# Queries in a pool of their own, column sums behind their conversions, and only the sums kept in DRAM: one change to a hybrid attention and SSD layer

## The chip, the core and the metric

The kernel runs on one core of a Trainium2 chip. The metric is the device time of that core in microseconds; a time stands for the median of several executions, and one further execution was taken with the profiler. The engines are named as in the profile: PE (matmul, with PEld for its weight loads), DVE (vector), ACT (scalar), POOL (GpSimd) and SP, which here only issues transfers. ACT and POOL issue transfers too, in the order of their other instructions.

## The reference

One decoder layer over x of 2048 positions by 1024 columns, in float32. A single projection gives queries, keys, values, two gates, the input of a convolution, and the step sizes of the SSD. Sixteen heads of causal attention with ALiBi bias are taken over windows of 128 steps at dilations 1, 4 and 16; beside them runs a Mamba-2 SSD scan over chunks of 128. Both branches are gated, normalized, put side by side and projected back:

```python
proj = jnp.einsum('bsd,de->bse', x, w_in[layer])
q, k, v, z_att, z_ssm, xbc, dt_raw = jnp.split(proj, list(SPLITS), axis=-1)
...
y_att = rms_norm(y_att.reshape(Bsz, S, D_ATT) * jax.nn.silu(z_att), att_norm_g[layer])
xbc = jax.nn.silu(causal_depthwise_conv(xbc, conv_w[layer], conv_b[layer]))
...
y = ssd_chunked(xs_h, dt, a, bm, cm) + d_skip * xs_h
y_ssm = rms_norm(y * jax.nn.silu(z_ssm), ssm_norm_g[layer])
out = jnp.einsum('bse,ed->bsd', jnp.concatenate([y_att, y_ssm], axis=-1), w_out[layer])
x = layer_norm(alpha * x + out, ln_g[layer], ln_b[layer])
```

## The kernel before

**Precision.** A float32 product is made of three matmuls: each operand is split into a high part (rounded to the faster fp32r type by ACT) and the rest (a subtraction on POOL or DVE), and high by high, high by low and low by high are summed in PSUM.

**Stages.** First the values are projected (L122 to L214). Then comes the product phase (L590 to L703), about half of the time: all other columns of the projection, and between them the convolution, the SSD and preparations for later. The attention follows (L706 on), eight pairs of heads, each over three dilations; last comes the output projection with the norm.

**The product phase.** It uses a Strassen-like scheme. A *job* is a block of 256 columns by one half of the tokens, and `products` (L289) makes it from seven products instead of eight; each product is 12 matmuls of 128x512. The token side has seven combinations of quarters of x (`LEFT`, L85), each a high and a low tile of 1 MB, read by `token_side` (L221) from DRAM; all fourteen lie in SBUF and change only when the half changes. The column side has seven combinations of the weight's quarters A11, A12, A21, A22: `column_load` (L234) brings the raw quarters (256 KB each) into tiles `wr`, `column_side` (L247) forms sums in place (`tt`, L250, on DVE) and splits each of the seven (`two`: the cast on ACT, L254, and the subtraction on POOL, L255) into a tile `w` of 512 KB. The order of the seven is A11, S1 = A21 + A22, A12, the new A11, the new A12, A22, A21; numbers 1, 3, 4 and 6 of them, counted from 0, are sums. Pool `wp` has seven `w` tiles, so a new one fits when the product that reads the old one is done.

There are 44 jobs in three phases: 10 with the first half of the tokens (phase 0: convolution inputs "c" and SSD gates "s"), 22 with the second half (phase 1: the same, and from job 19 on queries "q", keys "k" and attention gates "z", the list `rest`), and 12 with the first half again (phase 2: `rest`). The columns of phase 2 were used in phase 1, so there `column_side` stores its seven tiles into `d_wc` (L257, on SP), and in phase 2 `column_reload` (L269) reads all seven back (L274, on POOL) without ACT or DVE.

**The order.** PE, DVE, ACT and POOL run in the order of the program text. `products` calls `flush` after each product; `after(n, f)` puts work n flushes ahead, so a *step* is one product. Columns of the next job are prepared from step 2 to step 8, the raw quarters of the one after next loaded at steps 3, 4, 6 and 7. `keep` (L301, L303) copies a product from PSUM on ACT, `put` (L306, L311) adds on DVE, and `fin` stores or goes on one step later. PSUM has five tiles `pp` for this, four used by a job.

Other work hangs on the same steps: `sums_part` (L103) forms the token combinations of the second half in jobs 0 to 3; `wout_load` (L639) brings pieces of the output weight, split three steps later by `split_w` (L115) into two buffers `wot` and stored on SP; `copy_v` (L477) rearranges the values in DRAM; in phase 1 `conv_tile` (L376) reads a convolution input `U` (two buffers) at step 0 and 3 of its job, `conv_steps` (L392) runs it on ACT (L397), DVE (three taps, L400) and ACT (L406). From job 23 on 32 SSD units (chunk, group) are placed at `spots` (L615): 13 of them 63/13 steps apart, then 19 at 4.1 steps. A unit has six stages, a step each: `ssd1` (L497) transposes on PE, masks the product of B and C with `tri` on DVE (L507), makes eight ramps on ACT (L513) and then copies B's transpose on ACT (L517); `ssd2` (L519) takes the exponential and multiplies by the mask; the last ones are matmuls and gates, and `d_us` is stored (L576).

**Memory.** Pools grow from both sides of SBUF. On the right, the SSD's tiles (`sd`, 36 KB a partition) follow the convolution's. When the product phase ends, the attention's pools lie over them: on the right `qk0` and `qk1`, the keys of two pairs of heads (16 KB each), on the left `io`, with the queries (`qh`, `ql`) first, which puts them over the `w` tiles. `load_qk` (L724) reads queries and keys, high and low, on POOL's queue in the order qh, kh, ql, kl.

## Time and profile before

| | us |
|---|---|
| median of three runs | 2279.07 (2272.51 to 2279.48) |
| the profiled execution | 2279.57 |
| its span, first to last instruction | 2277.8 |
| values projected until | 209.4 |
| product phase | 209.4 to 1336.3 |
| attention from | 1353.8 |

The mean granted clock of PE over the span is 0.948. The page gives, for each engine, its busy time and the number of its instructions; the stretches give the same for a part of the span; the waits name the engine and line that stood still, what released it, the total, how often, and the longest. A row with L255 means line 255 of the kernel; a row with "<-" in its tiles reads as out <- in. Idle time of an engine is a cost only where the chain that ends last runs through it.

### The profile page before, as it was taken

To read this page: it belongs to the slowest core of one execution; us is meant where nothing else is said; L and a number is where in the kernel's file an instruction comes from. 1 tells how busy PE (TensorE), PEld (TensorE's weight loads), DVE (VectorE), ACT (ScalarE), POOL (GpSimd) and SP (SyncE) were. 2 spreads that over 40 slices of the span, in tenths; PEclk is the share of its full clock that TensorE was granted. 3 is DMA by queue.
4 is the path that set the end of the run, shared out by engine and by line. 5 is a ranking of instruction groups with operands and counts; after the bars stand their busy time and mean duration, and the time that the engine had idled before them with its cause. 6 is when DMAs were issued, how large, how long until landed. Compare 5 with 4: busy or idle time off the path is not lost.

```text
span 2277.8 us, 38897 instructions
## 1 busy us (share of the span) xinstructions
PE 2088.7 (92%) x13824; PEld 1729.8 (76%) x13824; DVE 1368.8 (60%) x3141; ACT 1132.2 (50%) x2967; POOL 1017.3 (45%) x815
## 2 busy tenths in 40 slices
PE   7999789879898899988999979999999985999998
PEld 7998667657777677766888858888888864888886
DVE  3421554437778667743555537888888865565554
ACT  3321443325445566643655637888888861222221
POOL 2113343446565565653444431366677771232221
PEclk9999889989999999998999978999999997999999
DMA  9989666876667999899999973577777799422220
GB/s 333 367 313 334 229 230 240 294 297 197 206 207 254 331 358 342 322 364 386 292 316 303 304 257 120 162 199 211 220 218 219 218 318 273 152 99 100 80 91 35
DMA packets 280561, 557.51 MB, mean 245 GB/s; under 512 B 45360, under 2 KB 136624, under 8 KB 264368
## 3 DMA queue, kind: packets, MB, share of 16 engines
q1 hardware_dynamic: 206496, 291.81, 39.8%
q0 software_dynamic: 35152, 173.03, 21.2%
q10 hardware_dynamic: 38720, 90.20, 12.3%
q8 instruction: 109, 1.79, 0.3%
q14 instruction: 84, 0.69, 0.1%
HBM read 357.42 MB, written 214.30 MB: 251 GB/s over the span
## 4 chain that ended last, share of the span: by engine, by line
PE 40%; DMA 12%; DVE 5%; ACT 4%; issue 2%; POOL 1%; ACTq 0%; SPq 0%; DVEq 0%; POOLq 0%
PE S L795 6%; PE N L844 6%; PE T L824 6%; PE S L1004 3%; PE S L1006 3%; PE S L1005 3%; DMA zt<-d_zs 3%; PE pp L294 2%; PE pp L296 2%; PE pp L298 2%; PE T L1004 2%; PE T L1005 2%; PE T L1006 2%; ACT P L811 1%; DVE P L803 1%
## 5 line engine op out<-in xcount | busy, mean ns | idle before, releaser
L255 POOL TENSOR_TENSOR w<-wr,w 128x512 fp32r<-128x512 f32 x224 | 354.3, 1599 | 282.4 <-ACT w L254 223.2
L811 ACT ACTIVATE P<-P,st 128x256 f32<-128x256 f32 (+1 forms) x768 | 345.1, 451 | 95.2 <-DVE st L803 94.4
L803 DVE CUSTOM_DVE_ANT_0 P<-S,tb 128x256 f32<-128x256 f32 (+1 forms) x768 | 235.2, 362 | 97.8 <-PE S L795 67.2
L826 DVE COPY PT<-T 128x512 f32<-128x512 f32 (+1 forms) x304 | 196.6, 677 | 1.5 <-PE T L824 1.5
L824 PE MATMUL T<-ident,P 128*128 128x128 f32 x1200 | 179.6, 287 | 5.9 <-DVE PT L826 5.9
L303 ACT COPY ev<-pp 128x512 f32<-128x512 f32 x176 | 102.2, 581 | 156.4 <-PE pp L298 103.6
L844 PE MATMUL N<-PT,v 128*64 128x128 f32 x2400 | 176.5, 284 | 0.0
L250 DVE TENSOR_TENSOR wr<-wr 128x512 f32<-128x512 f32 x128 | 129.9, 1015 | 71.9 <-POOL w L255 54.0
L254 ACT CAST w<-wr 128x512 fp32r<-128x512 f32 x224 | 136.2, 618 | 62.7 <-DVE wr L250 21.2
L844 PEld LDWEIGHTS N<-PT,v 128*64 128x64 f32 x2400 | 129.3, 138 | 33.3 <-issue 22.6
L824 PEld LDWEIGHTS T<-ident,P 128*128 128x128 f32 x1200 | 130.1, 142 | 30.8 <-DVE PT L826 7.3
L811 ACT ACTIVATION_READ_ACCUMULATOR P<-P,st 128x1 f32 x768 | 143.7, 187 | 0.0
L911 POOL TENSOR_TENSOR wb<-num,wb 128x2048 f32<-128x2048 f32 x21 | 96.3, 4586 | 100.1 <-DMA wb<-d_wd 58.8
L311 DVE TENSOR_TENSOR ev<-pp,ev 128x512 f32<-128x512 f32 x152 | 100.7, 682 | 60.8 <-PE pp L298 41.7
L795 PE MATMUL S<-kh,qp 64*128 64x256 f32 (+1 forms) x1024 | 126.4, 306 | 0.0
L981 DVE TENSOR_REDUCE tb<-P 128x128 f32<-128x1024 f32 x32 | 64.0, 2000 | 85.5 <-PE N L1010 45.3
L400 DVE SCALAR_TENSOR_TENSOR acc<-U,cw,acc 128x2048 f32<-128x2048 f32 x36 | 106.6, 2961 | 6.0 <-ACT acc L397 5.5
L294 PE MATMUL pp<-TT3h,w 128*128 128x512 f32 x176 | 78.0, 443 | 34.8 <-ACT ev L303 33.2
L795 PEld LDWEIGHTS S<-kh,qp 64*128 64x128 f32 x1024 | 88.8, 188 | 22.0 <-issue 20.9
L146 PE MATMUL pp<-vh,xh 128*128 128x256 f32 (+1 forms) x320 | 90.8, 290 | 14.5 <-ACT xh L169 14.5
L351 DVE SCALAR_TENSOR_TENSOR ev<-ev 128x512 f32<-128x512 f32 x64 | 60.2, 955 | 66.5 <-ACT ev L350 66.4
L513 ACT ACTIVATE mt<-csb,cs 128x128 f32<-128x128 f32 x256 | 78.5, 390 | 36.8 <-DMA csb<-d_cs 34.2
(362 smaller groups left out, 5994.5 us busy)
## 6 DMA issues: line engine op xcount, KB each, us to landing
d_wc<-w SPq DMA_DIRECT2D x84, 512.0 KB
w<-d_wc POOLq DMA_DIRECT2D x84, 512.0 KB, 7.4
wr<-w ACTq DMA_DIRECT2D x120, 256.0 KB
v<-d_v POOLq DMA_DIRECT2D x24, 1024.0 KB, 7.0
wb<-d_wd SPq DMA_DIRECT2D x48, 512.0 KB
csb<-d_cs ACTq DMA_DIRECT2D x32, 512.0 KB
st<-xT SPq DMA_DIRECT2D x31, 512.0 KB
d_v<-vt SPq DMA_DIRECT2D x16, 512.0 KB
```

Of the source, the lines that this page charges most:

```text
L250: tt = lambda o, a, b, op=OP.subtract: nc.vector.tensor_tensor(q[o], q[a], q[b], op=op)
L254: nc.scalar.copy(t[:, 0], q[nm])
L255: nc.gpsimd.tensor_tensor(t[:, 1], q[nm], t[:, 0].bitcast(F32), op=OP.subtract)
L294: nc.tensor.matmul(ps, w[:, 0, k], th[:, k], start=start and k == 0, stop=False, skip_group_check=not start)
L795: nc.tensor.matmul(ov(sp[h][:, 256 * b:256 * b + w]), A["q"][d][x][hr, blk], kv(A["k"][y][hr]), start=(m == 0), stop=(m == 2))
L803: nc.vector.tensor_tensor_reduce(P[:, h, b, 256 - w:256], sp[h][:, c0:c0 + w], tab[:, h, tab.shape[2] - w:], 1.0, 3.0e38, OP.add, OP.min, ...
L811: nc.scalar.activation(p, p, AF.Exp, bias=stat(A, 0, d, h, blk), scale=-1.0, accum_out=stat(A, 1, d, h, blk))
L824: nc.tensor.transpose(tp[:, h, b], P[:, h, b, 128 * which:128 * which + 128], ident)
L826: nc.vector.tensor_copy(pt[:, :, bl[0]:2], tp[:, :, bl[0]:2])
L844: nc.tensor.matmul(nm[64 * h:64 * h + 64, bq * 128:bq * 128 + 128], v[:, k, 64 * h:64 * h + 64], pts[which][:, h, b], start=(f or not whic ...
L1004: nc.tensor.matmul(ps, uh[:, e, :], wh, start=(e == 0), stop=False)
L1005: nc.tensor.matmul(ps, uh[:, e, :], wl, start=False, stop=False)
```

## The change

- `column_reload` reads only the four sums back from `d_wc`; the other three of a job (A11, A12, A22) are made from raw quarters as in `column_side`. So `column_load` runs for phase 2 too, with three quarters (`part`), on ACT's queue. `column_side` stores the sums alone.
- `column_side` has nine steps from step 0 on: A11 is converted at step 1 (2 before), A12 at step 2 (4 before); the in-place sums stay at steps 2, 4 and 5 and the other conversions where they were. `slot` takes the buffers in the old order. The four reloads come at steps 2, 4, 5 and 7 instead of 1, 3, 4 and 6.
- From job 11 on the first `conv_tile` of a job runs at step 5 of the job before.
- `sums_part` runs in jobs 1 to 4 instead of 0 to 3.
- `wot` has four buffers instead of two, and a piece of the output weight comes every 5/3 steps instead of 7/4.
- In the SSD, the copy of B's transpose moves in front of the ramps, and the masking from `ssd1` to `ssd2`; the later units stand 4 steps apart instead of 4.1.
- The queries get a pool `qq` on the right, between the two pools of keys, where the SSD's tiles lay.

```diff
-        def column_load(ct0, ct1, queue=nc.gpsimd):
+        def column_load(ct0, ct1, queue=nc.gpsimd, part=False):
...
+            if part:
+                return q, [lambda: load("A11", ct0, 0), lambda: load("A12", ct0, 1), lambda: load("A22", ct1, 1)]
             return q, [first, lambda: load("A12", ct0, 1), lambda: load("A22", ct1, 1), lambda: load("A21", ct1, 0)]
+
+        SUMS = (1, 3, 4, 6)
...
-            def two(nm):
-                t = wp.tile([128, 2, 4, 128], F32R, name="w")
+            def slot():
+                W.append(wp.tile([128, 2, 4, 128], F32R, name="w"))
+
+            def two(i, nm):
+                t = W[i]
                 nc.scalar.copy(t[:, 0], q[nm])
                 nc.gpsimd.tensor_tensor(t[:, 1], q[nm], t[:, 0].bitcast(F32), op=OP.subtract)
-                if save is not None:
-                    nc.sync.dma_start(d_wc[save, len(W)], t.bitcast(F32).rearrange("p a k c -> p (a k c)"))
-                W.append(t)
+                if save is not None and i in SUMS:
+                    nc.sync.dma_start(d_wc[save, i], t.bitcast(F32).rearrange("p a k c -> p (a k c)"))
...
-            steps = [[sums, lambda: two("A11")], [lambda: two("S1")],
-                     [lambda: tt("A11", "S1", "A11"), lambda: two("A12")],
-                     [lambda: tt("A12", "A12", "A11"), lambda: two("A11")],
-                     [lambda: two("A12")], [lambda: two("A22")], [lambda: two("A21")]]
+            steps = [[], [slot, lambda: two(0, "A11")], [sums, slot, slot, lambda: two(2, "A12")],
+                     [lambda: two(1, "S1")], [lambda: tt("A11", "S1", "A11")],
+                     [lambda: tt("A12", "A12", "A11"), slot, lambda: two(3, "A11")],
+                     [slot, lambda: two(4, "A12")], [slot, lambda: two(5, "A22")], [slot, lambda: two(6, "A21")]]
...
-        def column_reload(u):
+        def column_reload(u, q):
...
-            def two():
+            def step(i):
                 t = wp.tile([128, 2, 4, 128], F32R, name="w")
-                nc.gpsimd.dma_start(t.rearrange("p a k c -> p (a k c)"), d_wc[u, len(W)])
+                if i in SUMS:
+                    nc.gpsimd.dma_start(t.rearrange("p a k c -> p (a k c)"), d_wc[u, i])
+                else:
+                    nm = {0: "A11", 2: "A12", 5: "A22"}[i]
+                    nc.scalar.copy(t[:, 0], q[nm])
+                    nc.gpsimd.tensor_tensor(t[:, 1], q[nm], t[:, 0].bitcast(F32), op=OP.subtract)
                 W.append(t)
-            return W, [two] * 7
+            return W, [lambda: None] + [lambda i=i: step(i) for i in range(7)]
...
-            nc.vector.tensor_tensor(pb[:, 256:384], pb[:, 128:256], tri, op=OP.mult)
             if n < 15:
+                A["bs"] = bs = [sd.tile([128, 128], F32R, name=f"bs{p}", bufs=2) for p in "hl"]
+                nc.scalar.copy(bs[0], pb[:, 0:128])
                 A["xde"] = xde = sd.tile([128, 512], F32, name="xde")
...
-            if n < 15:
-                A["bs"] = bs = [sd.tile([128, 128], F32R, name=f"bs{p}", bufs=2) for p in "hl"]
-                nc.scalar.copy(bs[0], pb[:, 0:128])
...
             nc.scalar.activation(mt, mt, AF.Exp, scale=-1.0)
+            nc.vector.tensor_tensor(pb[:, 256:384], pb[:, 128:256], tri, op=OP.mult)
...
-        spots = [7 * 23 + 63 * i // 13 if i < 13 else 7 * 32 + (41 * (i - 13)) // 10 for i in range(32)]
+        spots = [7 * 23 + 63 * i // 13 if i < 13 else 7 * 32 + 4 * (i - 13) for i in range(32)]
...
-                after(3, lambda: split_w(j // 2, j % 2, raw, sums.tile([128, 2, 512], F32R, name="wot", bufs=2)))
+                after(3, lambda: split_w(j // 2, j % 2, raw, sums.tile([128, 2, 512], F32R, name="wot", bufs=4)))
             for j in range(16):
-                later.setdefault(7 * 5 + 1 + 7 * j // 4, []).append(lambda j=j: wout_load(16 + j))
+                later.setdefault(7 * 5 + 1 + 5 * j // 3, []).append(lambda j=j: wout_load(16 + j))
...
-                    for j in range(7):
-                        after(j + (0 if ph2 == 2 else 2), prep[j])
+                    for j, f in enumerate(prep):
+                        after(j, f)
...
-                if m + 2 < len(jobs) and jobs[m + 2][0] < 2:
-                    q2, steps_ = column_load(*cts[m + 2], nc.scalar)
+                if m + 2 < len(jobs):
+                    q2, steps_ = column_load(*cts[m + 2], nc.scalar, jobs[m + 2][0] == 2)
                     for n, f in zip((3, 4, 6, 7), steps_):
                         after(n, f)
+                if 10 < m + 1 < len(jobs) and jobs[m + 1][1][0] == "c":
+                    Un = [None]
+                    after(5, lambda i=jobs[m + 1][1][1], U=Un: (U.clear(), conv_tile(i, U)))
...
-                if m < 4:
+                if 1 <= m < 5:
                     for c in range(4):
-                        after(1 + c, lambda c=c, k=m: sums_part(sums, 1, k, raws[k], c))
-                    if m < 3:
-                        after(5, lambda k=m + 1: raws.__setitem__(k, sums_load(sums, 1, k)))
+                        after(1 + c, lambda c=c, k=m - 1: sums_part(sums, 1, k, raws[k], c))
+                    if m < 4:
+                        after(5, lambda k=m: raws.__setitem__(k, sums_load(sums, 1, k)))
...
-        qk = [c2.enter_context(tc.tile_pool(name=f"qk{i}", bufs=1, side="right", reuse_waits="tile"))
-              for i in range(2)]
+        qk = [c2.enter_context(tc.tile_pool(name="qk0", bufs=1, side="right", reuse_waits="tile"))]
+        qq = c2.enter_context(tc.tile_pool(name="qq", bufs=1, side="right", reuse_waits="tile"))
+        qk.append(c2.enter_context(tc.tile_pool(name="qk1", bufs=1, side="right", reuse_waits="tile")))
...
-                t = (io if x[0] == "q" else qk[pr % 2]).tile([128, NR, NJ], F32R, name=x, bufs=1)
+                t = (qq if x[0] == "q" else qk[pr % 2]).tile([128, NR, NJ], F32R, name=x, bufs=1)
```

## What the change will do, told before it was run

> **What bounds the kernel now.** I read the page's busy times first.
>
> ```profile
> PE 2088.7 (92%) x13824; PEld 1729.8 (76%) x13824; DVE 1368.8 (60%) x3141; ACT 1132.2 (50%) x2967; POOL 1017.3 (45%) x815
> ```
>
> TensorE leads, but a busy PE is not a PE at its peak, so the product phase was cut into stretches: the 44 jobs start where the timeline shows their first matmul on the tile TB11. The columns are the stretch, then busy time and instructions of PE, weight load, DVE, ACT and POOL, the granted clock, the DMA share and GB/s.
>
> ```profile
> 209.40:321.30 111.90, 90.18 (x342) 71.84 (x343) 60.13 (x92) 45.18 (x78) 46.69 (x38) 0.85 0.69 233
> 340.70:378.80 38.10, 38.10 (x170) 31.54 (x169) 15.96 (x19) 15.27 (x27) 16.25 (x12) 1.00 0.63 211
> 378.80:404.80 26.00, 22.01 (x85) 17.68 (x84) 12.12 (x12) 9.55 (x18) 11.20 (x8) 0.87 0.80 277
> 423.80:456.00 32.20, 24.10 (x86) 18.86 (x86) 13.26 (x13) 8.39 (x15) 14.28 (x16) 0.84 0.88 319
> 456.00:496.80 40.80, 27.47 (x86) 19.72 (x85) 8.00 (x11) 7.33 (x13) 14.96 (x18) 0.79 1.02 384
> 496.80:761.00 264.20, 240.99 (x1010) 193.56 (x1009) 206.72 (x163) 135.45 (x215) 158.16 (x94) 0.96 0.68 218
> 761.00:1004.00 243.00, 226.85 (x1184) 186.40 (x1182) 161.15 (x235) 156.77 (x317) 149.30 (x116) 0.96 0.93 337
> 1004.00:1058.50 54.50, 36.12 (x126) 25.88 (x125) 14.13 (x27) 16.60 (x35) 18.37 (x25) 0.75 1.08 413
> 1058.50:1292.10 233.60, 230.54 (x1301) 191.80 (x1300) 122.39 (x232) 136.42 (x281) 107.50 (x124) 1.00 0.93 304
> 1292.10:1317.00 24.90, 24.39 (x143) 20.15 (x141) 13.54 (x25) 13.21 (x29) 6.13 (x10) 1.00 1.09 369
> 1336.30:1353.80 17.50, 0.47 (x2) 0.32 (x3) 1.29 (x2) 1.23 (x2) 10.44 (x16) 0.58 1.00 370
> 1353.80:1385.60 31.80, 31.80 (x219) 25.38 (x220) 14.86 (x88) 19.21 (x84) 4.19 (x8) 0.50 0.19 70
> 1401.60:1433.40 31.80, 31.80 (x390) 26.59 (x388) 26.61 (x109) 24.37 (x96) 7.99 (x13) 1.00 0.22 72
> ```
>
> The second row is the yardstick: jobs 5 and 6 run without a gap, 38.1 / 2 = 19.05 us a job, 2.72 us a product. Job 42 (1292.1 to 1317.0) carries SSD units every 4.1 products, 7 / 4.1 = 1.71 of them, and takes 24.9: a unit costs PE (24.9 - 19.05) / 1.71 = 3.4 us. What a stretch takes beyond jobs and units is lost time:
>
> - jobs 0 to 3: 111.9 - 76.2 = 35.7
> - job 7: 26.0 - 19.05 = 7.0; job 9: 32.2 - 19.05 = 13.1; job 10, where all token tiles change: 40.8 - 19.05 = 21.8
> - jobs 11 to 22: 264.2 - 228.6 = 35.6
> - jobs 23 to 31 with 13 units: 243.0 - 171.5 - 44.2 = 27
> - job 32, the second change of token tiles: 54.5 - 19.05 - 5.8 = 30
> - jobs 33 to 41 with 15.4 units: 233.6 - 171.5 - 52.4 = 10
> - from the last product to the steady attention: 17.5
>
> Some 198 us, then, are in reach, 180 of them inside the phase of 1336.3 - 209.4 = 1127; the other 947 us of it are matmuls, and attention and output behind them are not touched. The waits say what ended the gaps (engine and line, releaser: total us, times, longest). Jobs 0 to 3:
>
> ```profile
> PE pp L294 <- ACT ev L303: 21.6, 4, 6.9
> DVE st L108 <- DMA st<-xT: 16.7, 2, 12.6
> ```
>
> Jobs 7 to 9:
>
> ```profile
> ACT wot L117 <- DMA d_wo<-wot: 42.5, 7, 12.5
> POOL w L255 <- ACT w L254: 36.5, 11, 8.5
> PE pp L294 <- ACT ev L303: 12.1, 3, 5.1
> POOL w L255 <- issue: 11.8, 2, 10.5
> ```
>
> Jobs 11 to 22:
>
> ```profile
> ACT U L406 <- DVE acc L400: 50.9, 10, 6.9
> DVE wr L250 <- POOL w L255: 39.8, 14, 6.3
> PE pp L294 <- ACT ev L303: 20.7, 10, 4.3
> ACT acc L397 <- DMA U<-d_cu: 20.4, 3, 7.5
> ```
>
> Everywhere PE waits for ACT's copy out of PSUM (L303), and ACT, which works in order, is stuck at something else: a store that has not landed, a convolution input, a DVE that itself waits for POOL.
>
> **The change part by part.**
>
> *Sums of the second token half, one job later.* No work is removed. Job 0 loses its four steps and with them the 12.6 us wait; the block then was loaded a whole job earlier. Job 4, clean until now, receives a set. Job 0's stall at its sixth product, some 8 us of its 11.7, goes; job 4 gets a stall like job 3's, 25.2 - 19.05 = 6 at most, and jobs 1 to 3 keep theirs. Bounds 0 and 12; near the middle I take **6 us**.
>
> *Output-weight staging, four buffers for two, a load every 5/3 products for 7/4.* The store of a buffer now has 4 x 1.67 x 2.72 = 18 us to land, against 9.5. A wait of at most 12.5 behind 9.5 means stores of up to 22, so most of the 42.5 us goes, not all. Job 7 gives 7. Job 9 gives up to 13; and since POOL hung on ACT in front of the token loads (10.5 us in the wait on "issue", where no releaser was found), those loads start earlier too. But they are fourteen tiles of 128x2048 fp32, 14.7 MB, at the 384 GB/s of job 10's row 38 us with nothing else to move: transfers take over there, and I give jobs 9 and 10 together 13 instead of 35. Sum **20 us**, bounds 5 and 34.
>
> *Convolution inputs from the step after the sixth product of the job before, not at the start of their own.* A lead of two products, 5.4 us, meets waits of at most 7.5 (20.4 us in three). The reset of the tile moves with it on POOL, and waits there for the store of the tile's last user; behind it on POOL are conversions that PE needs five products later. *In-place sums two products behind the conversions*: A11 is converted at step 1 instead of 2, A12 at 2 instead of 4, while the sums that overwrite them stay at 4 and 5. The 39.8 us that DVE spends on POOL here go; DVE is at 206.7 of 264.2 busy in this stretch and keeps ACT waiting 50.9 us (L406 on L400). What is late next is DVE itself. The new wait: A12's buffer comes free just as its cast is issued, so ACT can stand up to one product, 2.72 us, once a job; behind it is only the copy of the next product, which PE has not made yet. Bounds: 0 and the 35.6 lost; I take **14 us**, two fifths, since DVE's own load remains.
>
> *SSD and stores in jobs 23 to 31.*
>
> ```profile
> d_wc<-w SPq DMA_DIRECT2D x84, 512.0 KB
> w<-d_wc POOLq DMA_DIRECT2D x84, 512.0 KB, 7.4
> wr<-w ACTq DMA_DIRECT2D x120, 256.0 KB
> ```
>
> Of 84 stores 48 stay: 36 x 0.52 = 18.9 MB less of writing, in a stretch at 337 GB/s and share 0.93, which is 56 us of transfers over some thirteen jobs. The copy of B comes ahead of the eight ramps and no longer behind DVE's masking:
>
> ```profile
> ACT bsh L517 <- DVE ss L507: 14.4, 6, 3.8
> ...
> ACT ev L303 <- DMA xs<-d_xs: 7.7, 1, 7.7
> ```
>
> The 14.4 us go; the copy now waits for PE's transposes, which the ramps used to cover, about 1 us a unit, 13 in all if none is covered. The masking (289 ns on average) moves one step on DVE and costs the same. The second row is the kind of wait that fewer stores shorten: an ACT load held at issue. Bounds: -13, if the ramps' cover is lost and nothing comes back, and 27, all that is lost there; I take **8 us**, between the 1.4 that the two waits leave and the 15 midway to the top.
>
> *Job 32.* Its row shows 413 GB/s and a share of 1.08: transfers bound it. Of seven reloads three go (1.6 MB), three 0.26 MB loads come: 0.8 MB net, 2 us at 413 GB/s, up to 4 with the next job's set. Against it, three subtractions stand on POOL's queue between the token loads and wait for ACT's casts. **2 us**, bounds -6 and 8.
>
> *Jobs 33 to 43.* 36 reloads of 0.52 MB become 36 loads of 0.26 MB on ACT's queue, 36 casts and 36 subtractions:
>
> ```profile
> L255 POOL TENSOR_TENSOR w<-wr,w 128x512 fp32r<-128x512 f32 x224 | 354.3, 1599 | 282.4 <-ACT w L254 223.2
> ...
> L254 ACT CAST w<-wr 128x512 fp32r<-128x512 f32 x224 | 136.2, 618 | 62.7 <-DVE wr L250 21.2 <-DMA d_cu<-ev 19.1 <-DMA U<-d_cu 7.3
> ```
>
> 36 x 0.62 = 22 us on ACT and 36 x 1.6 = 58 on POOL, beside PE, which is 230.5 of 233.6 us busy there; ACT has 97 us free and POOL 126. The four reloads left come one product later but still five ahead of use, 13.6 us against a landing of 7.4. Units every 4 products instead of 4.1 end the SSD one product earlier, at no cost. What the held ACT loads cost can't be read from a row of this stretch; from -15 to 6, and I take **-2 us**, nearest to the quiet PE row.
>
> *Queries in their own pool.* The end of the products:
>
> ```profile
> 1320.49 0.32 SPq L576 DMA_DIRECT2D d_us<-xd  x1
> ```
>
> ```profile
> 1336.80 0.53 POOL L729 DMA_DIRECT2D qh<-d_qh  x1 [16.55 <-PE pp L298]
> ```
>
> ```profile
> PE S L795 <- DMA kh<-d_kh: 12.5, 1, 12.5
> ...
> PE S L795 <- DMA kl<-d_kl: 4.5, 1, 4.5
> ```
>
> Queries lay over the weight tiles, so POOL stood 16.55 us until the last matmul, and the keys, whose room was free, queued behind. Now all four loads (4.2 MB, 11 us at the 370 GB/s of that row) can follow the last SSD store at 1320.5, and end near 1335, before the products do. Of the 17.5 us, DVE's table and ACT's table load leave about 4: **13 us**, bounds 8 and 27 (below).
>
> **The sum.** 6 + 20 + 14 + 8 + 2 - 2 + 13 = 61. The profiled execution took 2279.57 (span 2277.8 and 1.8 around it), so 2279.6 - 61 = 2218.6; the median of the runs shown is 0.5 lower, 2279.07, and I say **2218 us**.
>
> **The rivals.** *More: the attention starts at full clock.* From 1353.8 to 1385.6 the clock was 0.50 and the row counts 219 matmuls; a later stretch of equal length at 1.00 has 390. The same work at full clock takes 219 / 390 x 31.8 = 17.9, so 13.9 us more could be had if PE does not go cold in the gap: about 2204. Against it: scores of two steps fill the banks, then PE waits some 3 us for tables and exponentials. [...]
>
> *Less: the waits only change their names.* In jobs 11 to 31 DVE's load and the loads held on ACT take over, and the 22 us of the two middle terms come to nothing: 2240. For it: 206.7 of 264.2 us of DVE. Against it: the same DVE gets 39.8 us of waits back.
>
> *Slower: ACT held at its new loads.* In phase 2 ACT now issues 36 more loads in a stretch at share 0.93, and each can hold the copies out of PSUM behind it.
>
> ```profile
> ACT ev L350 <- DMA d_kh<-ev: 14.5, 2, 7.5
> ```
>
> Waits of ACT on stores do occur here. ACT's spare is 97 us, the casts take 22; a hold of w a load passes to PE from w = 75 / 36 = 2.1 us, and eats the whole gain at (75 + 61) / 36 = 3.8. At 5 us it is 180 - 75 = 105 lost: 2279.6 - 61 + 105 = 2324. Against it: PE hardly waits there now, and there is 10% less to move.
>
> *It does not do what it says.* If the token loads and PE's pace set the phases whatever ACT does, only job 0 and some of the transition are left, 5 us: 2275.
>
> **How the numbers follow.** Forecast as summed (2195 to 2245 with its terms off by half) 0.52; full clock and more 0.18; names changed 0.16; slower 0.08; nothing 0.06. A measurement of this kernel tells about 0.3%, 7 us, from no change. The seven terms lie 6, 15, 14, 21, 8, 13 and 5 us above their low ends and 6, 14, 22, 19, 6, 8 and 14 below their high ones; added as squares, since they hang on different waits, that is 34 and 37 us: 2253 and 2182. The third case with the last two low ends of phase 2 (8 and 13) reaches 2261. So 2180 to 2262, with the slower case and the empty one left out. Faster 0.86, within 0.06, slower 0.08.
>
> **What would show it.** The wait of L117 on its store gone or below 10 us, jobs 7 and 9 near 19 and 22; DVE's wait for L255 gone and jobs 11 to 22 below 255 us; POOL's 16.55 us in front of qh gone and scores within 5 us of the last product; job 32 still near 50. ACT waits on DMAs in front of L303 in phase 2, or PE below 0.95 busy there, would prove me wrong; so would a convolution stretch that keeps its 264 us.

## The result, and the profile after

The changed kernel takes **2207.89 us** (median of three runs, 2201.86 to 2213.46) against 2279.07; the ratio is 0.9696, with an interval of 0.9647 to 0.9745. The forecast was 2218, 10 us too slow and on the right side. The profiled execution took 2207.89 as well, its span 2206.1.

The page's busy times, and its transfers of columns:

```profile
PE 2058.6 (93%) x13824; PEld 1712.9 (78%) x13824; DVE 1375.1 (62%) x3141; ACT 1153.3 (52%) x3003; POOL 1047.0 (47%) x815
...
wr<-w ACTq DMA_DIRECT2D x156, 256.0 KB
d_wc<-w SPq DMA_DIRECT2D x48, 512.0 KB
w<-d_wc POOLq DMA_DIRECT2D x48, 512.0 KB, 6.7
```

PE's matmuls are as many as before and take 30 us less, and as the clock is part of that (0.963 on average over the span, for 0.948), the stretches say more. Stores and reloads fell from 84 to 48, the raw quarters rose from 120 to 156, as the change says.

The stretches were cut as before, at the first matmul on TB11 of a job. The columns are the stretch, then busy time and instructions of PE, weight load, DVE, ACT and POOL, the granted clock, the DMA share and GB/s. The rows are jobs 0 to 4, 5 to 9, 10, 11 to 22, 23 to 31, 32 and 33 to 43 of the changed kernel, and the attention's start:

```profile
211.20:326.90 115.70, 104.57 (x427) 84.57 (x428) 62.86 (x96) 51.53 (x89) 54.50 (x45) 0.91 0.74 244
326.90:440.00 113.10, 99.96 (x422) 80.50 (x420) 44.14 (x57) 44.19 (x80) 49.41 (x40) 0.95 0.77 270
440.00:490.30 50.30, 28.90 (x85) 21.23 (x86) 9.84 (x15) 9.40 (x15) 15.90 (x19) 0.73 0.96 357
490.30:725.50 235.20, 231.01 (x1010) 190.21 (x1009) 213.47 (x162) 135.82 (x215) 163.10 (x93) 0.99 0.70 223
725.50:952.20 226.70, 218.34 (x1183) 180.12 (x1182) 161.74 (x239) 158.60 (x320) 152.54 (x118) 1.00 0.88 310
952.20:1004.30 52.10, 33.44 (x127) 25.60 (x126) 13.28 (x24) 18.23 (x38) 20.63 (x23) 0.74 1.06 401
1004.30:1279.30 275.00, 273.72 (x1526) 227.48 (x1524) 149.75 (x264) 171.91 (x348) 138.63 (x139) 1.00 0.86 280
1281.00:1312.80 31.80, 28.98 (x206) 22.92 (x204) 14.68 (x88) 19.37 (x84) 12.44 (x19) 0.54 0.43 141
```

Set beside the same cuts of before, in us:

| stretch | before | after | gain | forecast |
|---|---|---|---|---|
| jobs 0 to 4 | 131.3 | 115.7 | 15.6 | 6 |
| jobs 5 to 9 | 115.3 | 113.1 | 2.2 | with job 10: 20 |
| job 10 | 40.8 | 50.3 | -9.5 | |
| jobs 11 to 22 | 264.2 | 235.2 | 29.0 | 14 |
| jobs 23 to 31 | 243.0 | 226.7 | 16.3 | 8 |
| job 32 | 54.5 | 52.1 | 2.4 | 2 |
| jobs 33 to 43 | 277.8 | 275.0 | 2.8 | -2 |
| all after the last product | 941.5 | 926.8 | 14.7 | 13 |

Jobs 5 to 10 together lost 7.3 us where 20 were to be gained; jobs 0 to 4, 11 to 22 and 23 to 31 each gave about twice their term.

The waits of jobs 11 to 22 after the change (engine, line and tile, releaser: total us, times, longest):

```profile
ACT ev L315 <- PE pp L310: 44.5, 22, 3.3
...
ACT U L418 <- DVE acc L412: 27.5, 10, 4.3
...
DVE wr L254 <- POOL w L262: 1.2, 2, 0.6
```

DVE's wait for POOL fell from 39.8 us to 1.2, and the copy out of PSUM now waits for PE, 44.5 us, where PE used to wait 20.7 us for it; PE is busy 231.0 of 235.2 us and bounds this stretch.

At the end of the products, POOL's issue of the queries and keys, and PE's first scores:

```profile
1262.65 0.54 POOL L746 DMA_DIRECT2D qh<-d_qh  x1
1268.00 0.53 POOL L746 DMA_DIRECT2D kl<-d_kl  x1 [3.75 <-DMA d_us<-xd]
```

```profile
1279.27 0.33 PE L812 MATMUL S<-kh,qh 64*128 64x128 f32 x2
1280.72 0.33 PE L812 MATMUL S<-kl,qh 64*128 64x128 f32 x2 [1.12 <-DMA kl<-d_kl]
```

The 16.55 us in front of qh are gone: all loads start before the last product, and the scores follow it at once.

### The profile page after: what moved, and what is told of

It reads as the page before. It is cut to its first block, busy times and chain, and to the rows that moved or that the text cites. A ratio compares the mean times of both kernels' runs of the same rounds, so it can differ in the third digit from the quotient of the medians.

```text
span 2206.1 us, 38841 instructions
## 1 busy us (share of the span) xinstructions
PE 2058.6 (93%) x13824; PEld 1712.9 (78%) x13824; DVE 1375.1 (62%) x3141; ACT 1153.3 (52%) x3003; POOL 1047.0 (47%) x815
## 4 chain that ended last, share of the span: by engine, by line
PE 49%; DMA 14%; DVE 7%; ACT 5%; issue 4%; POOL 3%; ACTq 1%; SPq 0%; DVEq 0%; POOLq 0%
PE N L861 6%; PE S L812 6%; PE T L841 6%; PE pp L306 5%; PE pp L310 5%; PE pp L308 5%; PE S L1021 3%; PE S L1023 3%; PE S L1022 3%; PE T L1021 2%; PE T L1022 2%; PE T L1023 2%; DVE acc L412 2%; DMA U<-d_cu 2%; DMA zt<-d_zs 2%
## 5 line engine op out<-in xcount | busy, mean ns | idle before, releaser
L315 ACT COPY ev<-pp 128x512 f32<-128x512 f32 x176 | 102.3, 581 | 208.1 <-PE pp L310 121.0
L861 PEld LDWEIGHTS N<-PT,v 128*64 128x64 f32 x2400 | 129.2, 138 | 34.2 <-issue 22.6
L363 DVE SCALAR_TENSOR_TENSOR ev<-ev 128x512 f32<-128x512 f32 x64 | 66.6, 1054 | 64.1 <-ACT ev L362 64.0
L812 PEld LDWEIGHTS S<-kh,qp 64*128 64x128 f32 x1024 | 88.9, 188 | 22.0 <-issue 20.7
L412 DVE SCALAR_TENSOR_TENSOR acc<-U,cw,acc 128x2048 f32<-128x2048 f32 x36 | 101.3, 2813 | 3.1 <-ACT acc L409 2.6
L139 POOL TENSOR_TENSOR vl<-vraw,vh 128x256 fp32r<-128x256 f32 (+1 forms) x32 | 30.0, 940 | 131.7 <-ACT vh L138 110.0
L147 PE MATMUL pp<-vl,xh 128*128 128x256 f32 (+1 forms) x320 | 90.8, 288 | 0.0
```

The source lines that it names most:

```text
L412: return lambda: nc.vector.scalar_tensor_tensor(acc[0], U[:, j:j + 16, :], cw[:, i, j:j + 1], acc[0], op0=OP.mult, op1=OP.add)
L812: nc.tensor.matmul(ov(sp[h][:, 256 * b:256 * b + w]), A["q"][d][x][hr, blk], kv(A["k"][y][hr]), start=(m == 0), stop=(m == 2))
L861: nc.tensor.matmul(nm[64 * h:64 * h + 64, bq * 128:bq * 128 + 128], v[:, k, 64 * h:64 * h + 64], pts[which][:, h, b], start=(f or not whic ...
```

## The experiments

Each kernel is the changed one with one edit; its diff is against the changed kernel. A kernel's own time is a median, and the stretches are of its profiled execution. Two of the kernels below, whose edits turned out to do nothing, came to 2207.26 and 2207.61, which bears out 2207.9 as the mark to count from. It is not exact: the kernel before, timed again beside each group of runs, came to 2271.8 to 2279.1, so a few us between groups say little, and there the ratio to the kernel before and the stretches are the better guide. Stretches scatter as well: jobs 23 to 31 took 224.6 to 232.9 us, 228.7 on average, in the ten kernels (the changed one among them) whose edits leave them alone, and jobs 11 to 22 took 234.7 to 238.6.

### The queries back over the weight tiles

```diff
-                t = (qq if x[0] == "q" else qk[pr % 2]).tile([128, NR, NJ], F32R, name=x, bufs=1)
+                t = (io if x[0] == "q" else qk[pr % 2]).tile([128, NR, NJ], F32R, name=x, bufs=1)
```

(and the pool `qq` goes)

> The changed kernel with the queries back in the left pool. Theory: the loads were held by the weight tiles; without the new pool POOL waits some 16 us before qh again, and the time is 14 us above the changed kernel's 2207.9, near 2222, with the other phases as in the changed kernel. Rival, that the earlier end of the SSD alone lets the attention start earlier: within 4 us of 2207.9.

2216.8 us, ratio 0.9738 (0.9707 to 0.9768): 8.9 us worse. All after the last product took 936.4 against 926.8, so the pool is worth 9 to 10 us there. The waits of 1250 to 1310 us:

```profile
POOL ql L745 <- PE pp L310: 15.2, 1, 15.2
PE S L811 <- DMA kl<-d_kl: 10.9, 1, 10.9
```

POOL's wait comes back, but in front of ql and not of qh: of the four loads qh and kh were already through, which fits that only a part of the old gap returns: PE waits 10.9 us for kl here, and waited 12.5 for kh and 4.5 for kl before.

### The convolution input late again

```diff
-                if 10 < m + 1 < len(jobs) and jobs[m + 1][1][0] == "c":
+                if 99 < m + 1 < len(jobs) and jobs[m + 1][1][0] == "c":
```

> The changed kernel with the first convolution input of a job loaded at the start of its own job again. Jobs 11 to 22 took 264.2 us before and 235.2 after. Theory 'loads' (ACT's wait for the input at the head of its queue was the cause): the stretch goes back to 250 or more, the time to 2223 or more. Rival 'conversions' (DVE's wait for POOL was the cause): the stretch stays below 243, the time below 2216.

2207.26 us, 0.9701 (0.9679 to 0.9723); jobs 11 to 22 took 236.1 against 235.2. The earlier place is worth nothing that these runs can tell. The theory "loads" falls, and SP's timeline shows why: the place in the program did not make the read earlier. First the changed kernel, whose job 12 begins at 509.33, then this one, where it begins at 504.00 (a store of a finished input, and the read of the next into the same buffer):

```profile
506.67 0.37 SPq L424 DMA_DIRECT2D d_xs<-U  x1
515.10 0.92 SPq L391 DMA_DIRECT2D U<-d_cu  x2
```

```profile
501.34 0.37 SPq L424 DMA_DIRECT2D d_xs<-U  x1
509.22 0.92 SPq L391 DMA_DIRECT2D U<-d_cu  x2
```

The stores landed at 515.02 and 509.14, and the read follows each within 0.1 us, 5.8 and 5.2 us after the job's first matmul. With two buffers of U the read went out when the last user's store had landed, from either place.

### The conversions at their old steps

```diff
-            steps = [[], [slot, lambda: two(0, "A11")], [sums, slot, slot, lambda: two(2, "A12")],
-                     [lambda: two(1, "S1")], [lambda: tt("A11", "S1", "A11")],
+            steps = [[], [], [sums, slot, lambda: two(0, "A11")], [slot, lambda: two(1, "S1")],
+                     [lambda: tt("A11", "S1", "A11"), slot, lambda: two(2, "A12")],
```

> The changed kernel with A11 converted at step 2 and A12 at step 4 again, two steps closer to the sums that overwrite them. Theory 'conversions': DVE's wait for POOL comes back (40 us in jobs 11 to 22), the stretch goes to 250 or more, the time to 2223 or more. Theory 'loads': the stretch stays below 243, the time below 2216. If both this kernel and the one with the late load stay below 243, either part alone does it.

2230.47 us, 0.9803 (0.9776 to 0.9831): 22.6 us worse, the largest of all. Jobs 11 to 22 of this kernel, and their waits:

```profile
491.00:748.10 257.10, 240.00 (x1009) 191.48 (x1008) 207.50 (x163) 135.59 (x215) 156.34 (x94) 0.97 0.64 202
```

```profile
ACT U L418 <- DVE acc L412: 47.0, 11, 6.9
DVE wr L254 <- POOL w L262: 38.0, 10, 6.1
ACT acc L409 <- DMA U<-d_cu: 19.7, 3, 6.8
```

257.1 us is 21.9 more than after, and all three waits of before are there again, 38.0 us of DVE standing behind POOL first among them. The third was never a late read. The first of its three, with what DVE did just before it:

```profile
532.64 1.76 DVE L254 TENSOR_TENSOR wr<-wr 128x512 f32<-128x512 f32 x1 [5.32 <-POOL w L262]
534.33 0.22 DVE L398 COPY U<-U 128x127 f32<-128x127 f32 x1
534.63 2.01 ACT L409 ACTIVATE acc<-U,cw 128x2048 f32<-128x2048 f32 x1 [6.65 <-DMA U<-d_cu]
```

ACT waits for several semaphores here, and the profile names the last to change; the reads of this input had landed by 521.8. ACT begins 0.09 us after DVE's copy inside U, which came late because DVE had stood behind POOL. All three waits of this kernel named U, and all three of before, end so, 0.08 to 0.09 us after such a copy and 11 to 16 us after their reads had landed: they belong to the same jam.

### All seven column tiles stored and read back

```diff
-        SUMS = (1, 3, 4, 6)
+        SUMS = (0, 1, 2, 3, 4, 5, 6)
...
-                if m + 2 < len(jobs):
+                if m + 2 < len(jobs) and jobs[m + 2][0] < 2:
```

> The changed kernel, but all seven combinations of a job's columns are stored in DRAM in jobs 19 to 31 and all seven read back in jobs 32 to 43, as before the change; the rest is the changed kernel's. In the changed kernel jobs 23 to 31 take 226.7 us against 243.0 before, and jobs 32 to 43 327 against 332. Theory 'stores': the 16.3 us of jobs 23 to 31 came from 18.9 MB less of writing; with all stores back they take 240 or more and the kernel about 2222. Rival 'order': they came from the conversions' order and the copy of B ahead of the ramps; jobs 23 to 31 stay below 230 and the kernel within 5 us of 2208.

2220.24 us, 0.9749 (0.9727 to 0.9772), 12.4 worse. Jobs 11 to 22, whose last four already store, and jobs 23 to 31:

```profile
485.80:728.80 243.00, 233.17 (x1009) 191.03 (x1008) 213.98 (x162) 135.97 (x215) 163.82 (x94) 0.99 0.74 237
728.80:962.80 234.00, 222.90 (x1184) 183.59 (x1183) 163.57 (x235) 156.96 (x317) 150.40 (x117) 0.98 0.97 354
```

7.8 us more in the first and 7.3 in the second (5.3 against the average of 228.7), with the DMA share back from 0.88 to 0.97 and 354 GB/s for 310. The time is the one that "stores" named; of the 16.3 us of jobs 23 to 31 it explains less than half. Jobs 32 to 43 stayed at 327.3.

### The SSD's old order

```diff
+            nc.vector.tensor_tensor(pb[:, 256:384], pb[:, 128:256], tri, op=OP.mult)
             if n < 15:
-                A["bs"] = bs = [sd.tile([128, 128], F32R, name=f"bs{p}", bufs=2) for p in "hl"]
-                nc.scalar.copy(bs[0], pb[:, 0:128])
...
+            if n < 15:
+                A["bs"] = bs = [sd.tile([128, 128], F32R, name=f"bs{p}", bufs=2) for p in "hl"]
+                nc.scalar.copy(bs[0], pb[:, 0:128])
...
-            nc.vector.tensor_tensor(pb[:, 256:384], pb[:, 128:256], tri, op=OP.mult)
```

> The changed kernel, but in the SSD the copy of B's transpose stands behind the eight ramps again and the masking in the first stage, as before the change. Theory 'order': with the wait of the copy on DVE's masking back (14.4 us in jobs 11 to 31 before), jobs 23 to 31 take 234 or more against 226.7 and the kernel 2215 or more. Rival 'cover': the ramps hid the transposes, so the old place costs as much as it gains; jobs 23 to 31 stay within 3 us of 226.7 and the kernel within 4 of 2208.

2214.76 us, 0.9723 (0.9694 to 0.9751), 6.9 worse. Jobs 23 to 31 and 33 to 43, and the copy's wait in the first of these stretches:

```profile
724.40:958.50 234.10, 221.71 (x1183) 182.67 (x1183) 159.93 (x240) 158.63 (x320) 153.66 (x118) 0.99 0.84 299
1010.60:1290.90 280.30, 275.62 (x1526) 228.49 (x1524) 147.20 (x264) 171.75 (x348) 138.36 (x139) 0.99 0.84 275
```

```profile
ACT bsh L529 <- DVE ss L519: 16.3, 8, 3.4
```

7.4 us in jobs 23 to 31 and 5.3 in jobs 33 to 43. Against the average of 228.7, stores and order are worth 5.3 and 5.4 us of the 14.3 by which that average lies below the 243.0 of before; the rest of it is not attributed.

### Token sums from job 0

```diff
-                if 1 <= m < 5:
+                if m < 4:
```

(and the indices with it)

> The changed kernel, but the token sums of the second half are formed in jobs 0 to 3 again, not 1 to 4. In the changed kernel jobs 0 to 4 take 115.7 us against 131.3 before, where I had forecast a gain of 6. Theory 'one job later': all of it comes from the move; jobs 0 to 4 go back to 129 to 133 and the kernel to about 2223. Rival 'order of the conversions': half or more of the 15.6 comes from elsewhere (the conversions two steps earlier, or the buffers); jobs 0 to 4 take at most 124 and the kernel at most 2216.

2212.64 us, 0.9715 (0.9691 to 0.9739), 4.7 worse: the net gain is near the 6 of the forecast. Jobs 0 to 4 took a little more than the 124 that the rival allowed and less than the 129 of the theory. Jobs 0 to 4 and 5 to 9:

```profile
210.90:336.00 125.10, 106.83 (x427) 85.98 (x428) 66.37 (x102) 52.80 (x92) 54.10 (x45) 0.89 0.70 236
336.00:444.60 108.60, 99.19 (x422) 80.61 (x420) 42.18 (x54) 43.54 (x78) 49.38 (x40) 0.95 0.79 274
```

Moving the sums gains 9.4 us in jobs 0 to 4 and gives 4.5 back in jobs 5 to 9: job 5 takes 19.0 here and 23.0 in the changed kernel, where the last set runs into it (20.3 to 23.0 in the other kernels). With job 10 (48.6) jobs 5 to 10 took 157.2 here, against 156.1 before and 163.4 in the changed kernel: of the 7.3 us lost there, 6.2 go with the sums. The other 6.2 of the 15.6 us are not theirs, and the conversions aren't it either (118.0 with the old ones). Nearly all of them lie in job 3 (25.2 before, 19.4 here); what made it shorter stays open.

### Two buffers for the output weight

```diff
-                after(3, lambda: split_w(j // 2, j % 2, raw, sums.tile([128, 2, 512], F32R, name="wot", bufs=4)))
+                after(3, lambda: split_w(j // 2, j % 2, raw, sums.tile([128, 2, 512], F32R, name="wot", bufs=2)))
...
-                later.setdefault(7 * 5 + 1 + 5 * j // 3, []).append(lambda j=j: wout_load(16 + j))
+                later.setdefault(7 * 5 + 1 + 7 * j // 4, []).append(lambda j=j: wout_load(16 + j))
```

> The changed kernel with two buffers for the split output weight and a piece every 7/4 steps. Jobs 5 to 9 took 115.3 us before and 113.1 after, job 10 took 40.8 and 50.3. Theory 'traffic' (four buffers took ACT's wait away, but the transfers only move, and job 10 pays): jobs 5 to 10 together as in the changed kernel within 6 us, the time within 6 us of 2207.9. Rival 'buffers' (they gain what was forecast, and job 10 is longer for another reason): jobs 5 to 10 longer by 12 or more, the time above 2219.

2210.94 us, 0.9724 (0.9698 to 0.975). Jobs 5 to 9, and job 10:

```profile
326.30:450.20 123.90, 105.25 (x421) 84.65 (x420) 51.19 (x62) 44.67 (x80) 51.37 (x43) 0.92 0.76 265
450.20:492.40 42.20, 24.51 (x85) 18.65 (x85) 8.55 (x9) 6.66 (x12) 13.45 (x16) 0.76 1.01 372
```

123.9 + 42.2 = 166.1, against 113.1 + 50.3 = 163.4. Four buffers gain 10.8 us ahead of job 10, and job 10 gives 8.1 back. What ACT waits for instead is in its timeline of the changed kernel, in job 9 (start, duration, engine, line, operation; in brackets the idle time before and its releaser; ACTq is its queue for transfers):

```profile
424.45 0.34 ACTq L652 DMA_DIRECT2D woraw<-wout  x1
424.83 0.62 ACT L261 CAST w<-wr 128x512 fp32r<-128x512 f32 x1 [9.36 <-DMA d_cu<-ev]
```

The cast does not need the convolution's store `d_cu`. It stands behind the issue of the next piece's read, and that one, out at 424.45, was held until the store had landed, at 424.38: the wait in front of a split has become one in front of a read.

### The convolution inputs out of the token switch

In job 10 of the changed kernel ACT stands 26.7 us, named a wait for U:

```profile
ACT ev L315 <- DMA U<-d_cu: 26.7, 1, 26.7
```

```diff
+                if m == 9:
+                    after(2, swap)
+                    Un = [None]
+                    after(5, lambda U=Un: (U.clear(), conv_tile(0, U), conv_tile(1, U)))
```

(`swap` opens the pool of U in the middle of job 9, not at its end)

> The changed kernel, but the first two convolution inputs of phase 1 are read in job 9 (their pool opens at step 2 of it, the reads are issued at step 5), ahead of the fourteen token tiles and not between them. In the changed kernel job 10 takes 50.3 us, and ACT's copy out of PSUM (L315) stands there 26.7 us, by the trace behind a transfer of U. Theory 'held issue': ACT's weight load is held by the completion of a U read that is stuck in the token reads; without it job 10 takes 40 us or less and the kernel about 2198. Rival 'traffic': job 10 is bound by its 14.7 MB of token tiles; ACT's wait goes to another transfer, job 10 stays at 47 or more and the kernel within 4 us of 2208.

2207.61 us, 0.9687 (0.9662 to 0.9712); job 10 took 48.6. This run did not test its theory: SP still issued the reads behind its stores, at 442.0 us for 443.2, and ACT's wait was 26.7 us again. But it gives a floor. The last token tile of the run:

```profile
458.04 0.53 POOL L229 DMA_DIRECT2D TT3l<-d_T1T  x1 [2.77 <-DMA TB21l<-d_T1B]
```

```profile
TT3l<-d_T1T POOLq DMA_DIRECT2D x1, 1024.0 KB, 21.7
```

It landed at 458.0 + 21.7 = 479.7 and the job had begun at 439.4, so with its reads as they ran here job 10 can't end much before 43 us, whatever ACT does. The next run puts the same reads on POOL's queue, ahead of the token tiles:

```diff
+                    after(3, lambda U=Un: (U.clear(), conv_tile(0, U, nc.gpsimd), conv_tile(1, U, nc.gpsimd)))
```

> The changed kernel, but the first two convolution inputs of phase 1 are read on POOL's queue at step 3 of job 9, ahead of the token tiles that stand on the same queue (SP issued them at 443 us still in the run before this one, behind its stores, so that they lay between the token reads all the same). Theory 'held issue' of which a part is left: the token tiles end at 480 us in that run, so job 10 can't be much below 43 us; without ACT's wait of 26.7 us it takes 42 to 45 against 48.6 to 50.3. Rival 'traffic alone': ACT waits for another transfer instead, and job 10 stays at 47 or more.

2203.78 us, 0.9701 (0.9679 to 0.9724), and job 10 at 50.2. ACT's timeline there:

```profile
466.22 0.33 ACTq L240 DMA_DIRECT2D wr<-w  x1
466.60 0.59 ACT L315 COPY ev<-pp 128x512 f32<-128x512 f32 x1 [20.72 <-POOL w L262]
```

SP's read of U is out of the way, and ACT still stands 20.7 us in front of the issue of a column weight. By the trace's records it waited for a store of SP's until 453.2, and from then to 466.2 for POOL's subtraction to be done with the tile that the weight goes into. POOL was late with that, because the reads of U stood on its own queue now, each held until an earlier read had landed:

```profile
458.13 0.55 POOL L392 DMA_DIRECT2D U<-d_cu  x1 [2.93 <-DMA TB21l<-d_T1B]
464.92 1.27 POOL L262 TENSOR_TENSOR w<-wr,w 128x512 fp32r<-128x512 f32 x1
```

The changed kernel reached this subtraction at 445.4. So the edit took one hold away and made another. Job 10 kept its time, as "traffic alone" had it; that the traffic alone sets it is not shown.

### Without the second half of the output weight

```diff
-                later.setdefault(7 * 5 + 1 + 5 * j // 3, []).append(lambda j=j: wout_load(16 + j))
+                pass
...
-            nc.gpsimd.dma_start(t, d_wo[e].rearrange("p a c -> p (a c)"))
+            nc.gpsimd.dma_start(t, d_wo[e % 8].rearrange("p a c -> p (a c)"))
```

> The changed kernel without the staging of the second half of the output weight in jobs 5 to 9: its 16 pieces are neither read nor split nor stored, and the output projection reads the first half's pieces in their place. In the changed kernel jobs 5 to 9 take 113.1 us where 95.3 would be clean, and job 10 takes 50.3. Theory 'staging': the pieces cost what is left there; jobs 5 to 9 fall to 100 or less and job 10 to 45 or less. Rival 'token switch': the losses come from the stores of the convolution's input and from the token tiles; jobs 5 to 9 stay at 108 or more and job 10 within 3 us of 50.

2185.01 us in the one run taken. Jobs 5 to 9, and job 10:

```profile
326.00:425.00 99.00, 97.15 (x422) 79.92 (x421) 32.69 (x45) 35.49 (x64) 48.47 (x41) 0.98 0.63 214
425.00:466.00 41.00, 26.82 (x85) 18.88 (x84) 7.35 (x12) 9.91 (x15) 16.38 (x20) 0.83 0.95 365
```

140.0 us for 163.4: the staging costs **23.4 us** after the change, or 20 counted from the 160.3 that the quickest of the other kernels with four buffers and the moved sums took for these jobs. Jobs 7 to 9 run clean here, at 19.0 each.

### PE kept busy at the attention's start

```diff
+        def keep_clock(A, n, pool, name):
+            ps = pool.tile([128, 512], F32, name=name)
+            kh = f2(A["k"][0])
+            for k in range(n):
+                nc.tensor.matmul(ps, kh[:, 0:128], kh[:, 128:640], start=True, stop=True)
...
+                    if i == 0:
+                        keep_clock(pairs[0], 6, psS, "S")
                     pts[i] = scores(pairs[pr], d, qd, half)
+                    if i == 1:
+                        keep_clock(pairs[0], 10, psT, "T")
```

(likewise 4 after the third step's scores and 16 ahead of the first values)

> The changed kernel with 36 matmuls of 128x512 more whose result nobody reads, on tiles of the first keys, at the attention's start: 6 ahead of the first scores, 10 after the second step's, 4 after the third's, 16 ahead of the first values, where PE stands idle for want of keys, tables and values. In the changed kernel the granted clock is 0.50 from 1281 to 1312.8, 31.8 us. Theory 'cold start': PE's short gaps at that place cost it the clock; with the gaps filled the clock stays above 0.9 and the rest of the kernel after the last product takes 914 us or so against 926.8, the kernel about 2196. Rival 'loads': the start waits for tables and values on their way from DRAM anyway; the clock is up, but the rest of the kernel stays within 4 us of 926.8. Third: the clock falls all the same, and the added matmuls cost 4 to 8 us.

**2195.8 us**, 0.9661 (0.9641 to 0.9682): 12 us below the changed kernel's 2207.9, with 36 matmuls more; by the ratios, 0.9661 against 0.9696, it is 8. The attention's start:

```profile
1282.00:1313.00 31.00, 31.00 (x327) 24.56 (x327) 22.92 (x126) 25.81 (x116) 13.76 (x23) 1.00 0.51 180
```

The clock is 1.00 where it was 0.54, and 327 matmuls, some 25 of them the added ones, run in a stretch that held 206; all after the last product took 917.0 us for 926.8. "Cold start" holds.

### The pieces read on SP's queue

On top of the run before:

```diff
-                raw = sums.tile([128, 512], F32, name="woraw", bufs=3)
-                nc.scalar.dma_start(raw, wout[j // 2 * 128:j // 2 * 128 + 128, j % 2 * 512:j % 2 * 512 + 512])
-                after(3, lambda: split_w(j // 2, j % 2, raw, sums.tile([128, 2, 512], F32R, name="wot", bufs=4)))
+                raw = sums.tile([128, 512], F32, name="woraw", bufs=4)
+                nc.sync.dma_start(raw, wout[j // 2 * 128:j // 2 * 128 + 128, j % 2 * 512:j % 2 * 512 + 512])
+                after(4, lambda: split_w(j // 2, j % 2, raw, sums.tile([128, 2, 512], F32R, name="wot", bufs=4)))
```

> The changed kernel with the 36 matmuls of the run before at the attention's start (2195.8 us), and the 16 pieces of the output weight read on SP's queue instead of ACT's, with four buffers and the split four products after the read instead of three. Without these pieces jobs 5 to 9 took 99.0 us and job 10 took 41.0, against 113.1 and 50.3 in the changed kernel; ACT's longest waits there (9.4, 6.9, 6.9 us) end together with the issue of such a read, which stood behind the landing of a store. Theory 'held reads': on SP, which does nothing else but issue, the reads hold nobody; jobs 5 to 9 take 105 or less, job 10 no more than 50, and the kernel 2188 or less. Rival 'traffic': the pieces cost by their 12.6 MB of transfers, or ACT is held by its column weights instead; jobs 5 to 9 stay at 110 or more and the kernel within 4 us of 2195.8. Third: SP, held in its turn, sends the stores of the convolution's input and the pieces late, PE and ACT wait for the split, and the kernel takes 2200 or more.

2198.44 us, 0.9651 (0.9634 to 0.9669): no different from 2195.8. Jobs 5 to 9, and job 10:

```profile
322.40:432.60 110.20, 100.67 (x421) 81.71 (x420) 49.30 (x58) 44.06 (x80) 50.86 (x40) 0.95 0.77 270
432.60:482.70 50.10, 26.51 (x85) 19.20 (x84) 9.65 (x12) 7.04 (x13) 15.43 (x18) 0.76 1.00 370
```

In job 9 ACT now stands in front of a column weight:

```profile
417.77 0.33 ACTq L240 DMA_DIRECT2D wr<-w  x1
418.15 0.59 ACT L315 COPY ev<-pp 128x512 f32<-128x512 f32 x1 [7.71 <-DMA d_cu<-ev]
```

"Held reads" falls: taking them off ACT's queue moves the stall and does not remove it. The pieces' 16 x 0.79 = 12.6 MB take 34 us at the 370 GB/s of the last row, an estimate of the same order as the 23.4 they cost. That it is their bytes and not another part of their handling was not tried by itself.

## Why the prediction came out as it did

Counted by what each undoing cost: sums 4.7, buffers 3.0, early U -0.6, conversions 22.6, fewer stores 12.4, SSD order 6.9, queries 8.9, together 57.9 of the 71.2 us. Beside these runs the kernel before took 2272.8 and 2277.0, which makes the whole 65 to 69 us, so 8 to 13 are left. By the stretches, 6.2 lie in jobs 0 to 4 and 5.1 behind the products (14.7 against the 9.6 of the undoing); what made those was not separated. That the sum came out near is in part luck: by the table the staging missed by 27 us, and jobs 0 to 4, 11 to 22 and 23 to 31 together gave 33 more than forecast.

*Sums one job later: right*, 4.7 for 6. The stall moved as told, only on to job 5 and not into job 4.

*Output-weight staging: this step failed.* The forecast took L117's wait of 42.5 us for a shortage of buffers, and gave 20 us for it. L117's wait on its store did go, but jobs 7 and 9 took 23.4 and 27.5, not 19 and 22. The forecast itself said that transfers take over in jobs 9 and 10, and then still credited them with 13; job 10 in fact gave back 8.1 of the 10.8 us gained ahead of it. With the sums where they were, jobs 5 to 10 took 157.2 us against 156.1 before: nothing gained. It should have asked what is held next once the buffers are there, with 12.6 MB still to move in front of 14.7 MB of token tiles. Buffers: 3.0 us, within what two such medians scatter; staging as a whole: 23.4.

*Conversions and early U: the first right with the size off, the second wrong.* The term of 14 should have been 22 for the conversions alone and 0 for the early read. "Two fifths, since DVE's own load remains" was the mistake: DVE is busy 213.5 of 235.2 us, and ACT still waits 27.5 us for it, but PE is busy 231.0: all these waits leave it only 4.2 us to stand, and the loss of 35.6 us that was read off the yardstick was a better measure than DVE's busy share. The early read failed in its mechanism: the lead of two products never came about, because the buffer was free only when the store from it had landed (at 515.02 in job 12, with the read out at 515.10), which the forecast saw for the reset on POOL and not for the read; and the 20.4 us of waits that it was to meet were DVE's, not U's.

*SSD and stores: sign right, size too small*, 8 for 16.3 in jobs 23 to 31 (14.3 by the average), and stores also gave 7.8 in jobs 11 to 22, which were counted in another term. The ramps' cover was lost as feared (-13): ACT's copy of B waits 10.5 us for PE's transposes in jobs 23 to 31 (L521 on L518) and 21.3 in jobs 33 to 43, where in the old order it waited 16.3 and 18.6 for DVE's masking. On balance PE gained all the same: the order gained 5.3 in jobs 33 to 43 too, where the forecast had nothing for it.

*Job 32 and jobs 33 to 43: right*, 2.4 and 2.8 for 2 and -2; less the 5.3 of the SSD's order the latter are -2.5. ACT does stand in front of its copies there (L315, 7.0 us for a store of `d_qh` and 6.1 for one of `d_kh`; 8.6 for `d_qh` before), which the forecast had named as a sign against it, but the slower rival did not occur: PE is busy 273.7 of 275.0 us in jobs 33 to 43.

*Queries: right*, 14.7 for 13, with 9.6 shown to be the pool's; the other 5.1 are open.

*The rival of a full clock* did not occur: the attention's start still has 0.54. That its 2204 lies nearer to 2207.9 than the forecast is chance, two terms of double size against one that failed. Its price was sound: 13.9 us foretold, 8 to 12 measured once PE was kept busy.

## What to carry to other kernels

When a wait on a buffer is removed, look for what the same engine issues next: here the wait on a store went and one of 9.36 us turned up in front of a read, and of the edits tried only leaving the transfers out helped, by 23.4 us. A wait named after a transfer can be another's: those named U in jobs 11 to 22 ended 0.08 to 0.09 us after a copy of DVE's, so look at what ended just before. Order in-place updates behind the last reader so that no engine stands in a chain of three; it was worth 22.6 us here, more than any buffer (8.9 and 3.0). And where a phase begins with short gaps on PE, try a few matmuls whose result nobody reads: here 36 of them cost less than the gaps, by 8 to 12 us.

## What the runs showed of the hardware

**The clock fell in a gap of 1.86 us and stayed down for 30.8.** In the changed kernel PE's idle time at the attention's start was short, and yet the clock fell and stayed down (the columns of the second fence are those of the stretches):

```profile
1284.03 0.89 PE L812 MATMUL S<-kh,qh 64*128 64x128 f32 x2 [1.86 <-DVE st L820]
```

```profile
1278.00:1283.50 5.50, 3.04 (x30) 2.25 (x29) 1.33 (x3) 2.51 (x3) 1.54 (x2) 1.00 1.02 346
1283.50:1314.30 30.80, 29.32 (x196) 23.23 (x196) 14.65 (x88) 18.02 (x83) 10.90 (x18) 0.50 0.36 120
```

PE had stood 1.12 us for kl (at 1280.7), and stood 1.86 us again from 1282.2; 1.4 us into this gap, at 1283.5, the clock fell to 0.50, and it stayed there to 1314.3, through 30.8 us in which PE is counted busy for 29.32. With the gaps filled, PE busy for all 31.00 us from 1282.0 to 1313.0, the clock stayed at 1.00, so what PE does in them decided here; what ended the half clock at 1314.3 no run shows.

**An engine's issue of a transfer waited for another engine's transfer.** In job 10 of the changed kernel ACT stood 26.7 us in front of a weight read that nothing in the program ordered behind U. In the trace's records that read waits for semaphore 106, which SP's read of U, issued at 443.6 us, had used last: that one had landed at 478.40, and the weight read went out at 478.48. When U went to POOL's queue, such a read waited until 453.2 for semaphore 110 instead, last used by a store that SP had issued at 430.9. In the records of the changed kernel SP's and ACT's transfers use the same eight semaphores (100 to 103, 105 to 107 and 110, each 97 to 111 times by SP and 33 to 47 times by ACT; POOL's have 111 to 118), so a slow transfer of SP's held an issue of ACT's, and everything behind it.
